# Differential attention scores: three matmuls over 64 rows for each of two maps, in place of two over 128

## The chip, the cores and the metric

The kernel runs on one core of a Trainium2 chip. The metric is the device time of one execution in microseconds (us). A profiled execution of the kernel before is shown beside its times: its span is the time from its first to its last instruction. TensorE is called PE, its weight loads PEld, VectorE DVE, ScalarE ACT, GpSimd POOL and SyncE SP.

## What is computed

The reference is one layer of a decoder trunk with 1024 tokens of width 1024: an RMS norm, one wide input projection, two causal branches of 8 heads each (retention and differential attention), a SiLU gate on each branch, a projection of each branch, a merge by sigmoid gates, and an output projection added to the input. Only the differential attention is touched:

```python
qd = rms_norm(q_d.reshape(B, S, DIFF_HEADS, 2, DIFF_DK), diff_q_norm_g[l])   # DIFF_DK = 64
kd = rms_norm(k_d.reshape(B, S, DIFF_HEADS, 2, DIFF_DK), diff_k_norm_g[l])
...
for i in range(S // Q_BLOCK):                                                # blocks of 128 queries
    ...
    s = jnp.einsum('bqhjd,bkhjd->bhjqk', qb, kb) - slopes[None, :, None, None, None] * dist
    s = jnp.where(dist >= 0, s, -jnp.inf)
    p = jax.nn.softmax(s, axis=-1)
    a = p[:, :, 0] - lam * p[:, :, 1]
    outs.append(jnp.einsum('bhqk,bkhe->bqhe', a, vb))
```

Each head has two score maps, j = 0 and 1. Each is a product of queries and keys over 64 components, and the second softmax is subtracted from the first.

## The kernel before

**Stages.** The input is normalised and transposed, overlapping the first projections; then come the retention branch (to about 293 us), the differential attention (about 293 to 765 us), and the large gate and output products (to the end). All of it runs on one core, and TensorE works on independent pieces of several steps at a time.

**Precision.** A product of two float32 values is made from float32r matmuls. Each operand is split into a high part, rounded to float32r, and a low part, the remainder. The list `PASSES = ((0, 0), (0, 1), (1, 0))` names the three products that are kept: high by high, high by low, low by high.

**The differential stage.** It loops over 8 heads `h` and 8 tiles `t` of 128 queries, 64 steps in all. In a step, `dproj` projects a tile to queries, keys and values: 24 matmuls 384 columns wide into a PSUM bank `z_d` (line 121). The smaller pieces of earlier steps are handed to `after(d, w, fn, key)`: they are issued `d` steps later, between the parts of that step's projection, in the order of `key` (0 to 1 over the step), with `w` as their weight in the spacing. The tile framework then orders the instructions of each engine by a simulated timeline. The pieces of a tile are:

- `mean`, `scale`, `high`, `low` (one step later): the norm of queries and keys and the split. The tile `sp` (named `nsp`) has for each of four 64-wide pieces (query of map 0, query of map 1, key of map 0, key of map 1) the high part in columns 0 to 63 and the low part in columns 64 to 127.
- `d_qkT` (one step later): four transposes of `sp` into one `tr` bank `tq` (line 510). Transposed, rows 0 to 63 hold the high part and rows 64 to 127 the low part of one piece. ACT copies the queries three times into `Q` (lines 514 to 516): as they are, and with the halves exchanged, which needs two copies over 64 rows. DVE copies the keys into the head's `K` (line 517).
- `d_score` (two steps later): for one map `j` and one range of `m` columns of keys (tiles 0 to 3 have one range, tiles 4 to 7 have two), two matmuls over 128 rows into an `s` bank `sps` (line 533). The first adds high by high and low by low, the second, with the halves of the query exchanged, low by high and high by low. DVE adds the distance term and keeps the minimum (line 535), and after the last range ACT takes the exponential (line 539).
- `d_mix` (three steps later), then `d_aT` and `d_pv` (four steps later): the difference of the two maps, its transposes in `tr` banks (`aT`, line 560, copied to `aTs` on ACT or DVE, line 562), and its product with the values (`dops`, line 573). Then `d_norm` and `d_out`, the latter with four more transposes into a `tr` bank (line 610) for each four tiles.

PSUM has eight banks. `NPJ, NS, NTR` share seven of them out to the projections (`pj`), the scores (`s`, also used by retention) and the transposes (`tr`, also used by the first stages); the tag `o` has one.

Of the kernel before, what the change touches and what calls it, by code (L numbers as in the profile page):

```python
# [9 lines left out]
F32 = mybir.dt.float32  # L10
F32R = mybir.dt.float32r
AF = mybir.ActivationFunctionType
ALU = mybir.AluOpType
AX = mybir.AxisListType

P = 128
D = 1024
S = 1024
# [9 lines left out]
FMAX = 3.4028235e38  # L28
NWS = 11
TLS = True  # L30
QSB, KVB = 1, 1
NPJ, NS, NTR = 2, 2, 3
D_F, K_F = (1, 2, 2, 4), (.3, .3, .8, .5)
LAG_S, LAG_PV = 2, 4
K_N = (.1, .25, .4, .55)
D_MIX, K_MIX = 1, .05
K_QK, K_S, L_S, K_PV, L_PV = .9, 0., .8, .1, .8
# [25 lines left out]
def tile_hybrid_block(ctx, tc, x, norm_g, w_in, ret_norm_g, ret_w_o, dq_g, dk_g,  # L63
                      lq1, lk1, lq2, lk2, sub_g, diff_w_o, w_out, consts, out):
    nc = tc.nc
# [11 lines left out]
    def pst(tag, name, bufs=None):  # L77
        bufs = bufs or dict(pj=NPJ, s=NS)[tag]
        return ps.tile([P, 512], F32, tag=tag, name=name, bufs=bufs)
# [7 lines left out]
    def rstd(out_t, ss, pool, name, n, m):  # L87

        ms = pool.tile([P, n], F32, tag="rs_ms", name=f"ms_{name}", bufs=2)
        nc.gpsimd.tensor_scalar(ms, ss, m, EPS, ALU.mult, ALU.add)  # L90
        nc.gpsimd.tensor_tensor(out_t, ms, mh[:, :n], ALU.pow)  # L91
# [5 lines left out]
    def after(d, w, fn, key=1):  # L97

        later.setdefault(clock[0] + d, []).append((w, fn, key))

    PASSES = ((0, 0), (0, 1), (1, 0))
# [140 lines left out]
    def proj(chunk, t, n=512):  # L242
        if t == 3:
            wnext(chunk)
        z = pst("pj", f"z_{chunk}_{t}")
        step(z[:, :n], [hT[k, t // 4] for k in range(NK)], slice((t % 4) * P, (t % 4 + 1) * P),
             W[chunk], slice(0, n))
        return z
# [212 lines left out]
    with tc.tile_pool(name="dp", bufs=2) as dp:  # L461
        ndist = dp.tile([P, S], F32, name="ndist", bufs=1)
# [3 lines left out]
        def dproj(h, t):  # L466
            if t == 0:
                gh = dp.tile([P, 4, 64], F32, tag="gh", name=f"gh{h}")
                nc.gpsimd.tensor_copy(gh[:, 2:4, :], gains[:, 2:4, :])
                nc.gpsimd.tensor_scalar(gh[:, 0:2, :], gains[:, 0:2, :], 2.0 ** (h - 2), None, ALU.mult)  # L470
                heads[h] = dict(V=[], Q={}, sp={}, S={}, st={}, aT={}, o={}, O={}, g=gh)
            hd = heads[h]
            z = proj(f"d{h}", t, 384)
            if t % 4 == 0:
                hd["V"].append(dp.tile([P, 4, P], F32, tag="V", name=f"V{h}{t}", bufs=3))
            zqk = z[:, :256].rearrange("p (a b) -> p a b", b=64)
            sq = dp.tile([P, 4, 64], F32, tag="nsq", name=f"nsq{h}{t}")
            nc.scalar.activation(sq, zqk, AF.Square)
            nc.scalar.activation(hd["V"][t // 4][:, t % 4, :], z[:, 256:384], AF.Copy)  # L479
            ss = dp.tile([P, 8], F32, tag="nss", name=f"nss{h}{t}")  # L480
            sp = hd["sp"][t] = dp.tile([P, 4, P], F32R, tag="nsp", name=f"nsp{h}{t}")

            def mean():
                nc.vector.tensor_reduce(ss[:, :4], sq, AX.X, ALU.add)
                rstd(ss[:, 4:], ss[:, :4], dp, f"n{h}{t}", 4, 1.0 / 64)

            def scale():
                nc.vector.tensor_tensor(sq, zqk, ss[:, 4:].unsqueeze(2).broadcast_to([P, 4, 64]),  # L488
                                        ALU.mult)
                nc.gpsimd.tensor_tensor(sq, sq, hd["g"], ALU.mult)  # L490


            def high():
                nc.scalar.activation(sp[:, :, 0:64], sq, AF.Copy)

            def low():
                nc.vector.tensor_tensor(sp[:, :, 64:128], sq, sp[:, :, 0:64].bitcast(F32),
                                        ALU.subtract)

            for i, fn in enumerate((mean, scale, high, low)):  # L500
                after(1, .01, fn, K_N[i])

        def d_qkT(h, t):
            hd = heads[h]
            sp = hd["sp"].pop(t)
            if t == 0:
                hd["K"] = dp.tile([P, 2, S], F32R, tag="K", name=f"K{h}")
            tp = pst("tr", f"tq{h}{t}", NTR)
            for i in range(4):
                nc.tensor.transpose(tp[:, i * P:(i + 1) * P].bitcast(F32R), sp[:, i, :], identr)  # L510
            tv = tp.rearrange("p (a b) -> p a b", b=P)

            Q = dp.tile([P, 2, 2, P], F32R, tag="Q", name=f"Q{h}{t}", bufs=3)
            nc.scalar.activation(Q[:, :, 0, :], tv[:, 0:2, :], AF.Copy)
            nc.scalar.activation(Q[0:64, :, 1, :], tv[64:P, 0:2, :], AF.Copy)
            nc.scalar.activation(Q[64:P, :, 1, :], tv[0:64, 0:2, :], AF.Copy)  # L516
            nc.vector.tensor_copy(hd["K"][:, :, t * P:(t + 1) * P], tv[:, 2:4, :])
            hd["Q"][t] = Q

        def d_score(h, t, j, f, m):  # L520

            hd = heads[h]
            n = (t + 1) * P
            slope = 2.0 ** -(h + 1)
            if j == 0 and f == 0:
                hd["st"][t] = dp.tile([P, 8], F32, tag="ast", name=f"ast{h}{t}", bufs=5)
            if f == 0:
                hd["S"][t, j] = dp.tile([P, S], F32, tag=f"S{j}", name=f"S{h}{t}{j}", bufs=3 - j)
            st, sb = hd["st"][t], hd["S"][t, j]
            c = slice(m * f, m * f + m)  # L530
            sp = pst("s", f"sps{h}{t}{j}{f}")
            for e in range(2):
                nc.tensor.matmul(sp[:, :m], hd["Q"][t][:, j, e, :], hd["K"][:, j, c],  # L533
                                 start=(e == 0), stop=(e == 1))
            nc.vector.tensor_tensor_reduce(  # L535
                sb[:, c], sp[:, :m], ndist[:, S - n + m * f:S - n + m * f + m], -slope,
                FMAX if f == 0 else st[:, j:j + 1], ALU.add, ALU.min, st[:, j:j + 1])
            if m * f + m == n:
                nc.scalar.activation(sb[:, :n], sb[:, :n], AF.Exp, bias=st[:, j:j + 1], scale=-1.0,  # L539
                                     accum_out=st[:, 2 + j:3 + j])  # L540

        def d_mix(h, t):

            hd = heads[h]
            n = (t + 1) * P
            st, S0, S1 = hd["st"][t], hd["S"][t, 0], hd["S"].pop((t, 1))
            nc.vector.reciprocal(st[:, 4:6], st[:, 2:4])
            nc.vector.scalar_tensor_tensor(st[:, 6:7], st[:, 2:3], st[:, 5:6], nlam,
                                           ALU.mult, ALU.mult)
            nc.vector.scalar_tensor_tensor(S0[:, :n], S1[:, :n], st[:, 6:7], S0[:, :n],  # L550
                                           ALU.mult, ALU.add)
# [54 lines left out]
        def d_out(h, f):  # L606
            O = heads[h]["O"].pop(f)
            tp = pst("tr", f"oT{h}{f}", NTR)
            for b in range(4):
                nc.tensor.transpose(tp[:, b * P:(b + 1) * P], O[:, b, :], ident)  # L610
            oT = dp.tile([P, 512], F32, tag="oT", name=f"doT{h}{f}", bufs=1)
            nc.scalar.activation(oT, tp, AF.Copy, scale=gcol[:, 1, h:h + 1])
            nc.sync.dma_start(ot_d[h][:, f * 512:(f + 1) * 512], oT)

        for h in range(H):
            for t in range(NT):
                dproj(h, t)
                nf = (t + 4) // 4
                after(1, .34, lambda a=(h, t): d_qkT(*a), K_QK)
                for j in range(2):  # L620
                    for f in range(nf):
                        m = (t + 1) * P // nf
                        after(LAG_S, m / 1200, lambda a=(h, t, j, f, m): d_score(*a),
                              K_S + L_S * (j * nf + f) / (2 * nf))
                after(LAG_S + D_MIX, .01, lambda a=(h, t): d_mix(*a), K_MIX)
                nbs = [min(4, t + 1 - 4 * f) for f in range(nf)]
                seq = [(d_aT, f, .116 * nbs[f]) for f in range(nf)]
                seq += [(d_pv, f, .218 * nbs[f]) for f in range(nf)]
                for i, (fn, f, w) in enumerate(seq):
                    after(LAG_PV, w, lambda fn=fn, a=(h, t, f): fn(*a), K_PV + L_PV * i / len(seq))  # L630
                if t % 4 == 3:
                    for i in range(3):
                        after(LAG_PV + D_F[i], .01, lambda a=(h, t // 4, i): d_norm(*a), K_F[i])
                    after(LAG_PV + D_F[3], .46, lambda a=(h, t // 4): d_out(*a), K_F[3])
                tick()
# [345 lines left out]
```

## Time and profile before

| what | value |
|---|---|
| time, median of 3 runs | 1322.15 us (1320.63 to 1325.82) |
| profiled execution, its own time | 1322.55 us |
| its span | 1320.8 us |
| mean granted TensorE clock | 0.985 |
| instructions | 19793 |
| HBM traffic, mean | 128 GB/s |

How to read what follows. In a row of a group, the source line, engine and operation are followed by the output and inputs by their tile names, shapes and count; after the first bar stand the busy time in us and the mean length of one in ns; after the second, the engine's idle time just before them and what ended it. Matmuls are pipelined and their ends are modelled, so a matmul's length is longer than its distance to the next. The chain that ended last is followed back from the last instruction, at each step to what released it or to the instruction before it on its engine.

### The profile page before, as it was taken

What the parts mean: (1) busy time and instruction counts of PE and PEld (TensorE: products, weight loads), DVE (VectorE), ACT (ScalarE), POOL (GpSimd) and SP (SyncE); (2) the same over time, 40 slices, a digit from 0 to 9 for tenths busy, and PEclk for the clock granted to TensorE, in tenths of its full rate; (3) what the DMA queues carried; (4) which work ended last, traced back from release to release, by engine and by line L of the source; (5) the groups of instructions that cost most, each with busy time, mean ns of one, the idle gap of its engine ahead of it and who ended that gap; (6) DMA issues with size and microseconds to landing.
All of it is one profiled execution on the core that took longest, in us unless ns stands there. A gap on an engine that the chain in (4) does not pass through costs nothing.

```text
span 1320.8 us, 19793 instructions
## 1 busy us (share of the span) xinstructions
PE 1264.3 (96%) x6836; PEld 1113.4 (84%) x6836; DVE 950.9 (72%) x2016; ACT 651.4 (49%) x1448; POOL 265.4 (20%) x371
## 2 busy tenths in 40 slices
PE   7999999999999999999999997899989999998698
PEld 5888888889999999999999885687778888876586
DVE  7436435737786877777687838987876699998884
ACT  6235123527575766767676724434454454442420
POOL 3134113323333534243333100000000000012000
PEclk9999999999999999999999998899999999999799
DMA  7202120431010101102020326578876578998963
GB/s 259 66 29 72 57 72 8 125 107 49 9 57 9 57 10 56 55 11 65 9 72 9 120 89 201 189 256 276 298 251 208 160 245 274 301 277 178 253 191 112
DMA packets 157750, 169.95 MB, mean 129 GB/s; under 512 B 9921, under 2 KB 108369, under 8 KB 157649
## 3 DMA queue, kind: packets, MB, share of 16 engines
q1 hardware_dynamic: 154816, 163.68, 38.4%
q0 software_dynamic: 2832, 5.00, 2.6%
q8 instruction: 54, 0.88, 0.3%
q14 instruction: 48, 0.39, 0.1%
HBM read 122.51 MB, written 46.14 MB: 128 GB/s over the span
## 4 chain that ended last, share of the span: by engine, by line
PE 67%; DVE 13%; DMA 11%; issue 4%; ACT 3%; POOL 2%; SPq 1%; DVEq 0%; ACTq 0%; POOLq 0%
PE z_d L121 18%; PE z_rv L121 7%; PE z_rqk L121 6%; PE fb L130 5%; PE sps L533 5%; PE dops L573 5%; PE z_h L130 3%; PE w_h L130 3%; PE aT L560 2%; DMA og<-c_h 2%; PE X_out L130 2%; PE z_out L130 2%; PE w_out L130 2%; PE y_h L130 1%; DMA r_o<-og 1%
## 5 line engine op out<-in xcount | busy, mean ns | idle before, releaser
L121 PE MATMUL z_d<-w_d,hT 128*128 128x384 f32 x1536 | 303.5, 340 | 1.4 <-DVE nsq L488 1.4
L121 PEld LDWEIGHTS z_d<-w_d,hT 128*128 128x128 f32 x1536 | 264.3, 188 | 4.5 <-ACT V L479 1.7
L539 ACT ACTIVATE S<-S,ast 128x256 f32<-128x256 f32 (+7 forms) x128 | 99.0, 774 | 33.4 <-DVE ast L535 32.0
L533 PE MATMUL sps<-K,Q 128*128 128x512 f32 (+5 forms) x384 | 107.5, 363 | 0.5 <-ACT Q L516 0.5
L919 POOL DMA_DIRECT2D md<-c_y x16 | 13.9, 869 | 435.0 <-DVE ls_y L663 372.7
L121 PE MATMUL z_rv<-w_rv,hT 128*128 128x512 f32 x384 | 98.8, 397 | 0.0
L121 PE MATMUL z_rqk<-w_rqk,hT 128*128 128x512 f32 x384 | 94.1, 398 | 0.9 <-ACT hT L283 0.9
L121 PEld LDWEIGHTS z_rqk<-w_rqk,hT 128*128 128x128 f32 x384 | 70.9, 190 | 15.8 <-ACT hT L283 1.6
L573 PE MATMUL dops<-V,aTs 128*128 128x128 f32 x576 | 78.7, 275 | 0.0
L121 PEld LDWEIGHTS z_rv<-w_rv,hT 128*128 128x128 f32 x384 | 68.7, 188 | 11.8
L573 PEld LDWEIGHTS dops<-V,aTs 128*128 128x128 f32 x576 | 76.6, 191 | 2.2 <-ACT aTs L562 0.2
L535 DVE CUSTOM_DVE_ANT_0 S<-sps,ndist 128x512 f32<-128x512 f32 (+5 forms) x128 | 67.9, 533 | 10.4 <-PE sps L533 10.1
L130 PE MATMUL fb<-hT,fw 128*128 128x512 f32 x288 | 71.5, 396 | 0.0
L91 POOL TENSOR_TENSOR nss<-ms_n,mh 128x4 f32<-128x4 f32 x64 | 67.2, 1051 | 4.3
L533 PEld LDWEIGHTS sps<-K,Q 128*128 128x128 f32 x384 | 63.2, 189 | 3.1 <-ACT Q L516 1.5
L130 PEld LDWEIGHTS fb<-hT,fw 128*128 128x128 f32 x288 | 52.7, 188 | 10.2
L490 POOL TENSOR_TENSOR nsq<-nsq,gh 128x256 f32<-128x256 f32 x64 | 47.5, 746 | 63.7 <-DVE nsq L488 62.4
L550 DVE SCALAR_TENSOR_TENSOR S<-S,ast,S 128x128 f32<-128x128 f32 (+3 forms) x64 | 55.5, 868 | 1.2
L130 PE MATMUL z_h<-hT,ls_h 128*128 128x512 f32 x192 | 48.4, 401 | 6.0 <-DVE c_h L810 5.9
L130 PE MATMUL y_h<-t_h,ls_h 128*128 128x512 f32 x192 | 49.0, 398 | 3.3 <-ACT t_h L662 3.3
L662 ACT ACTIVATE ls_h<-s_h 128x512 fp32r<-128x512 f32 x64 | 38.6, 621 | 27.0 <-PE z_h L130 18.6
L130 PE MATMUL w_h<-t_h,l_h 128*128 128x512 f32 x192 | 48.4, 398 | 3.5 <-DVE u_h L822 3.5
(251 smaller groups left out, 2760.3 us busy)
## 6 DMA issues: line engine op xcount, KB each, us to landing
wr_d<-in_w_in_dram SPq DMA_DIRECT2D x96, 128.0 KB, 2.8
ra_h<-in_w_in_dram SPq DMA_DIRECT2D x16, 512.0 KB, 4.2
rb_h<-in_w_in_dram SPq DMA_DIRECT2D x16, 512.0 KB, 5.3
s<-sg SPq DMA_DIRECT2D x32, 256.0 KB, 4.2
fr<-in_w_in_dram SPq DMA_DIRECT2D x12, 512.0 KB, 4.8
first<-ft SPq DMA_DIRECT2D x24, 256.0 KB, 2.0
og<-c_h SPq DMA_DIRECT2D x24, 256.0 KB, 4.4
sg<-c_h SPq DMA_DIRECT2D x24, 256.0 KB, 3.3
```

The costliest lines, as they stand in the source:

```text
L91: nc.gpsimd.tensor_tensor(out_t, ms, mh[:, :n], ALU.pow)
L121: nc.tensor.matmul(o, a[k][:, i0, asl], b[k][:, i1, bsl], start=(k == 0 and j == 0), stop=(k == NK - 1 and j == 2))
L130: nc.tensor.matmul(bank, L[:, i0, j * P:(j + 1) * P], R[:, j, i1, :], start=(start and j == 0 and i == 0), stop=(j == 3 and i == 2), skip_ ...
L490: nc.gpsimd.tensor_tensor(sq, sq, hd["g"], ALU.mult)
L533: nc.tensor.matmul(sp[:, :m], hd["Q"][t][:, j, e, :], hd["K"][:, j, c], start=(e == 0), stop=(e == 1))
L535: nc.vector.tensor_tensor_reduce(sb[:, c], sp[:, :m], ndist[:, S - n + m * f:S - n + m * f + m], -slope, FMAX if f == 0 else st[:, j:j + 1 ...
L539: nc.scalar.activation(sb[:, :n], sb[:, :n], AF.Exp, bias=st[:, j:j + 1], scale=-1.0, accum_out=st[:, 2 + j:3 + j])
L550: nc.vector.scalar_tensor_tensor(S0[:, :n], S1[:, :n], st[:, 6:7], S0[:, :n], ALU.mult, ALU.add)
L560: nc.tensor.transpose(tp[:, b * P:(b + 1) * P], A[:, c:c + P], ident)
L573: nc.tensor.matmul(o[:, :P], aT[:, b, :], hd["V"][f][:, b, :], start=(kb == 0), stop=(kb == t))
L662: nc.scalar.activation(dst_hi, src, AF.Copy)
L919: nc.gpsimd.dma_start(m, t, accum_op=ALU.add)
```

## The change

The halves of the array's rows hold the two maps, where they held the high and the low part of one. `sp` is laid out so that a transposed tile has map 0 in rows 0 to 63 and map 1 in rows 64 to 127: one tile with the high parts and one with the low parts of the queries, and the same for the keys. `Q` is then one copy, half as large. A call of `d_score` covers both maps of a column range: it takes two `s` banks and issues six matmuls over 64 rows, alternating between map 0 in the lower half and map 1 in the upper half, three passes each; low by low is no longer computed. Then follow the reductions and, after the last range, the exponentials of both maps. `NS` goes from 2 to 3 and `NTR` from 3 to 2, and the weights given to `after` follow the new grouping.

```diff
-NPJ, NS, NTR = 2, 2, 3
+NPJ, NS, NTR = 2, 3, 2
...
+            sv = sp.rearrange("p (a h) (b c) -> p a h b c", h=2, b=2)
+            sqv = sq.rearrange("p (a b) c -> p a b c", b=2)
+
             def high():
-                nc.scalar.activation(sp[:, :, 0:64], sq, AF.Copy)
+                nc.scalar.activation(sv[:, :, 0], sqv, AF.Copy)
 
             def low():
-                nc.vector.tensor_tensor(sp[:, :, 64:128], sq, sp[:, :, 0:64].bitcast(F32),
-                                        ALU.subtract)
+                nc.vector.tensor_tensor(sv[:, :, 1], sqv, sv[:, :, 0].bitcast(F32), ALU.subtract)
...
-            Q = dp.tile([P, 2, 2, P], F32R, tag="Q", name=f"Q{h}{t}", bufs=3)
-            nc.scalar.activation(Q[:, :, 0, :], tv[:, 0:2, :], AF.Copy)
-            nc.scalar.activation(Q[0:64, :, 1, :], tv[64:P, 0:2, :], AF.Copy)
-            nc.scalar.activation(Q[64:P, :, 1, :], tv[0:64, 0:2, :], AF.Copy)
+            Q = dp.tile([P, 2, P], F32R, tag="Q", name=f"Q{h}{t}", bufs=3)
+            nc.scalar.activation(Q, tv[:, 0:2, :], AF.Copy)
...
-        def d_score(h, t, j, f, m):
+        def d_score(h, t, f, m):
...
-            sp = pst("s", f"sps{h}{t}{j}{f}")
-            for e in range(2):
-                nc.tensor.matmul(sp[:, :m], hd["Q"][t][:, j, e, :], hd["K"][:, j, c],
-                                 start=(e == 0), stop=(e == 1))
-            nc.vector.tensor_tensor_reduce(
-                sb[:, c], sp[:, :m], ndist[:, S - n + m * f:S - n + m * f + m], -slope,
-                FMAX if f == 0 else st[:, j:j + 1], ALU.add, ALU.min, st[:, j:j + 1])
+            sps = [pst("s", f"sps{h}{t}{j}{f}") for j in range(2)]
+            for i, (i0, i1) in enumerate(PASSES):
+                for j in range(2):
+                    b = slice(64 * j, 64 * j + 64)
+                    nc.tensor.matmul(sps[j][:, :m], hd["Q"][t][b, i0, :], hd["K"][b, i1, c],
+                                     start=(i == 0), stop=(i == 2))
+            for j in range(2):
+                sb = hd["S"][t, j]
+                nc.vector.tensor_tensor_reduce(
+                    sb[:, c], sps[j][:, :m], ndist[:, S - n + m * f:S - n + m * f + m], -slope,
+                    FMAX if f == 0 else st[:, j:j + 1], ALU.add, ALU.min, st[:, j:j + 1])
...
-                for j in range(2):
-                    for f in range(nf):
-                        m = (t + 1) * P // nf
-                        after(LAG_S, m / 1200, lambda a=(h, t, j, f, m): d_score(*a),
-                              K_S + L_S * (j * nf + f) / (2 * nf))
+                for f in range(nf):
+                    m = (t + 1) * P // nf
+                    after(LAG_S, m / 800, lambda a=(h, t, f, m): d_score(*a), K_S + L_S * f / nf)
```

More of the change, by code (lines that the diff above doesn't have):

```diff
@@ L524, in d_score @@
             slope = 2.0 ** -(h + 1)
-            if j == 0 and f == 0:
+            c = slice(m * f, m * f + m)
+            if f == 0:
                 hd["st"][t] = dp.tile([P, 8], F32, tag="ast", name=f"ast{h}{t}", bufs=5)
[L527 to L530, printed above, removed]
-            sp = pst("s", f"sps{h}{t}{j}{f}")
-            for e in range(2):
-                nc.tensor.matmul(sp[:, :m], hd["Q"][t][:, j, e, :], hd["K"][:, j, c],
-                                 start=(e == 0), stop=(e == 1))
-            nc.vector.tensor_tensor_reduce(
-                sb[:, c], sp[:, :m], ndist[:, S - n + m * f:S - n + m * f + m], -slope,
-                FMAX if f == 0 else st[:, j:j + 1], ALU.add, ALU.min, st[:, j:j + 1])
-            if m * f + m == n:
-                nc.scalar.activation(sb[:, :n], sb[:, :n], AF.Exp, bias=st[:, j:j + 1], scale=-1.0,
-                                     accum_out=st[:, 2 + j:3 + j])
+                for j in range(2):
+                    hd["S"][t, j] = dp.tile([P, S], F32, tag=f"S{j}", name=f"S{h}{t}{j}", bufs=3 - j)
+            st = hd["st"][t]
+            sps = [pst("s", f"sps{h}{t}{j}{f}") for j in range(2)]
[4 more added lines that the diff above has]
+                                     start=(i == 0), stop=(i == 2))
+            for j in range(2):
+                sb = hd["S"][t, j]
+                nc.vector.tensor_tensor_reduce(
+                    sb[:, c], sps[j][:, :m], ndist[:, S - n + m * f:S - n + m * f + m], -slope,
+                    FMAX if f == 0 else st[:, j:j + 1], ALU.add, ALU.min, st[:, j:j + 1])
+                if m * f + m == n:
+                    nc.scalar.activation(sb[:, :n], sb[:, :n], AF.Exp, bias=st[:, j:j + 1],
+                                         scale=-1.0, accum_out=st[:, 2 + j:3 + j])
         def d_mix(h, t):
```

## The prediction

> **What bounds the kernel now.** I read the page first: the engine totals, the chain that ended last, and the groups of the score lines.
>
> ```profile
> span 1320.8 us, 19793 instructions
> PE 1264.3 (96%) x6836; PEld 1113.4 (84%) x6836; DVE 950.9 (72%) x2016; ACT 651.4 (49%) x1448; POOL 265.4 (20%) x371
> PE 67%; DVE 13%; DMA 11%; issue 4%; ACT 3%; POOL 2%; SPq 1%; DVEq 0%; ACTq 0%; POOLq 0%
> L533 PE MATMUL sps<-K,Q 128*128 128x512 f32 (+5 forms) x384 | 107.5, 363 | 0.5 <-ACT Q L516 0.5
> L535 DVE CUSTOM_DVE_ANT_0 S<-sps,ndist 128x512 f32<-128x512 f32 (+5 forms) x128 | 67.9, 533 | 10.4 <-PE sps L533 10.1
> ```
>
> TensorE is busy nearly always and carries two thirds of the chain. The change touches the stage of the differential attention, from about 293 to 765 us, so the view by windows comes second, once for everything and once for the score tile `sps` alone.
>
> ```profile
> 293.00:765.00 472.00, 470.83 (x3090) 455.20 (x3089) 356.01 (x1031) 325.85 (x861) 166.14 (x243) 1.00 0.14 42
> 293.00:765.00 472.00, 107.48 (x384) 63.24 (x384) 108.99 (x192) 1.00 0.14 42
> ```
>
> The columns are length, PE, weight loads, DVE, ACT and POOL in the first row, and length, PE, weight loads and DVE in the second; then the granted clock (1.00), DMA share and GB/s. PE is busy 470.83 of 472 us, DVE 356, ACT 326. In this stage a microsecond of TensorE issue added or removed is a microsecond of the span, and work of DVE or ACT costs something only where a matmul waits for it.
>
> A matmul's busy time overlaps the next one's, so the price of one is the distance between them. I take that from the chain in order of time (start, length, what) and from the timeline of PE and of its weight loads (PEld), whose length of a merged row runs from the first start to the last end.
>
> ```profile
> 266.37 5.46 PE fb L130 x24
> 503.56 2.09 PE z_d L121 x12
> 508.32 0.35 PE sps L533 x2
> 494.53 0.30 PE sps L533 x2
> 527.92 0.24 PE sps L533 x2
> 505.65 0.89 PE dops L573 x8
> 531.11 0.30 PEld L533 LDWEIGHTS sps<-K,Q 128*128 128x128 f32 x2
> 503.23 2.10 PEld L121 LDWEIGHTS z_d<-w_d,hT 128*128 128x128 f32 x12
> 501.99 0.19 PEld L533 LDWEIGHTS sps<-K,Q 128*128 128x128 f32 x1 [0.36 <-ACT Q L516]
> ```
>
> 512 columns cost 5.46/24 = 0.227 us, 384 columns 2.09/12 = 0.174 us. The line through them gives 0.147 for 320, 0.20 for 448 and 0.12 for 256; the score pairs agree (384 wide 0.35/2, 320 wide 0.30/2). By the line 128 columns would cost 0.07, but they cost 0.12 in scores and 0.89/8 = 0.11 in `dops`. The weight load sets that: one load alone takes 0.19, two in a row span 0.30, so a second load follows 0.11 after the first. Where the stream is longer, loads keep its distance, (2.10 - 0.19)/11 = 0.174, and are hidden. So the price of a matmul today is the larger of its stream and 0.11 us.
>
> **The change part by part.** The counts come from the groups by shape, in the window of the stage.
>
> ```profile
> L533 PE MATMUL sps<-K,Q 128*128 128x512 f32 x96 | 32.7, 422 | 0.0
> L533 PE MATMUL sps<-K,Q 128*128 128x384 f32 x96 | 26.2, 361 | 0.5 <-ACT Q L516 0.5
> L533 PE MATMUL sps<-K,Q 128*128 128x448 f32 x64 | 19.2, 382 | 0.0
> L533 PE MATMUL sps<-K,Q 128*128 128x320 f32 x64 | 15.7, 322 | 0.0
> L533 PE MATMUL sps<-K,Q 128*128 128x256 f32 x32 | 7.5, 314 | 0.0
> L533 PE MATMUL sps<-K,Q 128*128 128x128 f32 x32 | 6.3, 284 | 0.0
> ```
>
> *1, matmuls and loads.* Before: 96 x 0.227 + 96 x 0.174 + 64 x 0.20 + 64 x 0.147 + 32 x 0.12 + 32 x 0.11 = 68.1 us. After, 384 matmuls of 128 rows become 576 of 64 rows: 288 couples, one matmul in rows 0 to 63 for map 0 and one in rows 64 to 127 for map 1, and there are 576 loads. Per width there are 3/4 as many couples as there were matmuls. All 6836 matmuls traced use 128 rows, so no row shows whether two of 64 rows run side by side. Bounds: wholly side by side, loads too, 3/4 of 68.1 = 51.1 us, a gain of 17.0; one after another, 6/4 of it = 102.1 us, a loss of 34.0. I take matmuls side by side (different rows, different PSUM banks) but loads in turn, by the nearest row: loads on one path 0.11 apart. Then a couple cannot cost less than two loads, 0.22 us, and only the 512 wide ones are bound by their stream: 72 x 0.227 + 216 x 0.22 = 63.9 us. Term: -4.2 us.
>
> *2, going into and out of 64 rows.* There are 96 groups of scores (8 heads, 4 tiles with one column range and 4 with two), each an island among 128-row matmuls: 192 changes, if the scheduler leaves the groups whole (each break adds two). Today a load is pulled under the running matmul. Whether a load for 64 rows is pulled under a matmul over all rows, and the reverse, no row shows. What one uncovered load costs does stand in the trace: the load at 501.99, late by 0.36 us, and the matmul it feeds, beside a matmul of the same 384 columns in the stream:
>
> ```profile
> 501.99 0.44 PE L533 MATMUL sps<-K,Q 128*128 128x384 f32 x1
> 501.44 0.34 PE L121 MATMUL z_d<-w_d,hT 128*128 128x384 f32 x1
> ```
>
> 0.44 - 0.34 = 0.10 us. Bounds per change: 0, if the load is pulled ahead as now; or 0.10 and the rest of the matmul in flight, 0.34 - 0.174 = 0.166, if the array must run empty first, 0.27 together. I take 0.10, the measured row. Term: 192 x 0.10 = +19.2 us, between 0 and +51.
>
> A rule of the Trainium skill speaks against this change. TensorEngine Tiling (Array Packing), Key Properties, says that changing the tiling mode, unlike changing the tile within a mode, drains TensorE. No row of before can show it; by it the term would be the upper end, +51.
>
> *3, the query copy.* Three ACT copies become one.
>
> ```profile
> L514 ACT ACTIVATE Q<-tq 128x256 fp32r<-128x256 f32 x64 | 24.8, 387 | 7.0 <-PE tq L510 6.8
> L515 ACT ACTIVATE Q<-tq 64x256 fp32r<-64x256 f32 x64 | 24.4, 382 | 0.9
> L516 ACT ACTIVATE Q<-tq 64x256 fp32r<-64x256 f32 x64 | 24.1, 377 | 0.8
> PEld sps L533 <- ACT Q L516: 1.5, 3, 0.6
> PE sps L533 <- ACT Q L516: 0.5, 2, 0.2
> PEld sps L533 <- ACT Q L514: 0.4, 1, 0.4
> ```
>
> ACT loses 24.4 + 24.1 = 48.5 us of work, all beside TensorE; Q is ready 0.76 us earlier. What matmuls wait for it is at most 1.5 + 0.5 + 0.4 = 2.4 us. Term: -2.4, at worst 0. The copies of the split (`high`, `low`) keep their counts and sizes: 0, hidden under PE.
>
> *4, PSUM banks.* `tr` falls from 3 to 2, so a transpose waits for the copy two before it. The trace has such waits with three banks: first the waits in total, then two pieces of the chain.
>
> ```profile
> PEld tq L510 <- ACT aTs L562: 1.7, 4, 0.4
> PE tq L510 <- ACT aTs L562: 0.7, 4, 0.2
> 501.97 0.59 ACT aTs L562
> 502.61 0.54 PE tq L510 x4
> ```
>
> Together 2.4 us. The bank of `tq` comes free 0.76 us sooner (part 3), and ready projection matmuls can fill a wait. I take a doubling, +2.4. Bounds: 0, and one wait of 0.59 in each of the 32 steps with two column ranges, +19. `s` rises from 2 to 3, but each call takes two at once: its second bank is one that the call before used, and the two reductions that free them now come together. PE has no visible wait for `s` today; a reduction takes 0.53 us (the L535 row) against the 2.9 us between two calls of a tile (0.4 of 472/64). The cover is that distance; gone, it would cost one reduction at most, in part of the 96 groups. I take 0. The DMAs, their sizes and the queues of SP and POOL are unchanged: 0.
>
> **Sum.** -4.2 + 19.2 - 2.4 + 2.4 = +15.0 us. The profiled execution took 1322.55 us (span 1320.8), 0.4 above the median 1322.15; so 1337.6 in its terms, **1337 us** for the median, 1.1% slower.
>
> **The rivals.**
>
> *Faster.* The loads of the two halves also go side by side and the changes cost next to nothing: -17.0 - 2.4 + 2.4, about 1305, or 1314 with 0.05 a change. For it: loads hide under matmuls everywhere today. Against: two loads are 0.11 apart. It decides at 17.0/192 = 0.089 us a change: below that the kernel gains, above it loses. The Trainium skill, TensorE: Matmul & The Clock Gate, Part 3, speaks for it: matmuls in different row groups start within about 4 ns, and loads overlap matmuls of another row group. No 64-row matmul runs here, so that is unseen.
>
> *No change.* One side of part 1 with the other of part 2: loads side by side but 0.10 a change, -17.0 + 19.2, 1324; or loads in turn and free changes, -4.2, 1318.
>
> *The array empties at every change.* 0.27 x 192 = 51, so 1369 with loads in turn and 1356 with loads side by side. For it: a matmul ends 0.166 after the next could start, so there is something to wait for. Against: nothing shown. The Trainium skill's sentence on draining, named in part 2 (TensorEngine Tiling (Array Packing), Key Properties), is the rule for this one.
>
> *No running side by side.* The change then does not do what it says: +34.0 by part 1, 1356, before any cost of changes. Against: the couples share neither rows nor banks. For: nothing in before has ever run so.
>
> **How the numbers follow.** Forecast with neighbours (1329 to 1350): 0.32. Faster: 0.31. No change: 0.15. Emptying array: 0.13. No running side by side: 0.09. Half a percent (6.6 us) is about what can be told from no change: faster 0.31, same 0.15, slower 0.32 + 0.13 + 0.09 = 0.54. The range must reach from the faster rival to the dearest ones: 1305 to 1370 leaves out under 0.2. The forecast's own range is 1329 to 1350.
>
> **What would show it.** Two score matmuls of a couple that start within hundredths of a microsecond show matmuls side by side; starts a stream apart show the last rival. Two score loads 0.11 apart on PEld confirm part 1's floor, and 384 wide couples then cost 0.22 of the chain, not 0.174. For part 2, the first 64-row matmul after a 128-row one, and the first 128-row one after, should last 0.10 longer than in the stream, or start that much late; nothing there means the faster rival, 0.27 the emptying one. For part 4, look at waits of transposes on `aTs` and `K`. The forecast is wrong above all if changes are free, or if loads of different rows do not queue.

## The result: 3.5% slower, and the profile after

The changed kernel takes 1367.91 us (median of 4 runs, 1365.46 to 1371.48) against 1321.39 for the kernel before on the same chip: ratio 1.0348, 95% interval 1.0314 to 1.0382, or 46.5 us lost. The forecast was 1337; the time lies inside the range, but the loss is three times the one forecast.

The page of the changed kernel, in the lines that answer to those of before (line 533 is now 535, 573 is 577, 560 is 564, 510 is 512), and behind them one row of the page of before:

```profile
span 1363.7 us, 19981 instructions
PE 1313.7 (96%) x7028; PEld 1110.7 (81%) x7028; DVE 947.7 (69%) x2016; ACT 601.1 (44%) x1320; POOL 266.4 (20%) x371
PE 73%; DVE 10%; DMA 10%; issue 3%; ACT 1%; POOL 1%; SPq 0%; DVEq 0%; POOLq 0%; ACTq 0%
L535 PE MATMUL sps<-K,Q 64*128 64x512 f32 (+5 forms) x576 | 107.9, 371 | 0.0
L535 PEld LDWEIGHTS sps<-K,Q 64*128 64x128 f32 x576 | 62.3, 184 | 29.0 <-issue 12.2
```
```profile
L533 PEld LDWEIGHTS sps<-K,Q 128*128 128x128 f32 x384 | 63.2, 189 | 3.1 <-ACT Q L516 1.5
```

ACT lost its 50 us of work, as the prediction said, and no gain of it shows. The busy time of the score matmuls is nearly unchanged (107.5 before, 107.9 now), although there are 576 instead of 384: a part of them overlap one another. New is the idle time of the load path before the score loads: 29.0 us, where it was 3.1 before. The largest part, 12.2 us, is put down to "issue", that is, to nothing the profile shows. Pieces of the chain, in order of time, show what it is.

```profile
523.38 0.17 PE z_d L121
523.56 0.64 PE sps L535 x3
525.79 0.72 PE sps L535 x5
527.80 0.44 PE dops L577 x4
528.25 0.72 PE sps L535 x3
528.97 0.64 PE dops L577 x4
```

The score pieces at 525.79 and 528.25 are both 384 columns wide. The first is a whole group of both maps (the chain counts five of its six matmuls), the second three matmuls of one map; both take 0.72 us. Three streams of 384 columns are 3 x 0.174 = 0.52, so each piece pays 0.20 on top. Whatever follows pays again: four `dops` matmuls take 0.64 behind the scores and 0.44 behind a projection. The timeline of PE and of its loads around the piece at 525.79:

```profile
525.28 0.19 PEld L121 LDWEIGHTS z_d<-w_d,hT 128*128 128x128 f32 x1
525.72 0.47 PEld L535 LDWEIGHTS sps<-K,Q 64*128 64x128 f32 x6 [0.25 <-issue]
526.43 0.42 PEld L614 LDWEIGHTS oT<-ident,O 128*128 128x128 f32 x4 [0.25 <-issue]
525.72 0.79 PE L535 MATMUL sps<-K,Q 64*128 64x384 f32 x6
```

Six matmuls over 64 rows go through in three streams, and six weight loads of 0.18 us lie within 0.47: the halves load and stream side by side. But the first load for 64 rows, and the first for 128 rows behind them, each come after 0.25 us in which the load path stood still. Before, loads were pulled under the running matmul.

I divided the distances between the ends of successive matmuls of the stage, all of them, from the first `z_d` to the last `fb`, into the stream (width price of the prediction, 0.11 us for 128 columns, the traced 0.072 for `tq`), what a matmul costs beyond it where the row count changes, and the other excess ("waits"). In us:

| kernel | other streams | score streams | changes: number, cost | waits | stage |
|---|---|---|---|---|---|
| before | 431.7 | 68.2 | 0 | 12.7 | 512.6 |
| after | 431.7 | 74.3 | 266, 49.0 | 7.2 | 562.2 |

The stage grew by 49.6: +49.0 for changes, +6.1 for score streams, -5.5 for waits. The span of the profiled execution grew by only 42.9, because after spent 520.6 us behind the stage where before spent 528.4. The experiments below spent between 523.6 and 531.0 there, apart from the three with one transpose bank (543 to 546); what moves this part, no run separates.

Two things beside the price went against the change. The scheduler did not keep the groups whole: in the program, 76 of the 133 runs of score matmuls hold three matmuls of one map alone, with projections, transposes or `dops` between the two maps. That makes 266 changes instead of 192, and only 163 of 288 couples side by side (ends within 0.024 us of each other).

### The profile page after: what moved, and what is told of

It is laid out like the page before. It is cut to its first block, busy times and chain, and to the rows that moved or that the text cites. A ratio compares the mean times of both kernels' runs of the same rounds, so it can differ in the third digit from the quotient of the medians.

```text
span 1363.7 us, 19981 instructions
## 1 busy us (share of the span) xinstructions
PE 1313.7 (96%) x7028; PEld 1110.7 (81%) x7028; DVE 947.7 (69%) x2016; ACT 601.1 (44%) x1320; POOL 266.4 (20%) x371
## 4 chain that ended last, share of the span: by engine, by line
PE 73%; DVE 10%; DMA 10%; issue 3%; ACT 1%; POOL 1%; SPq 0%; DVEq 0%; POOLq 0%; ACTq 0%
PE z_d L121 20%; PE sps L535 7%; PE z_rv L121 6%; PE z_rqk L121 6%; PE dops L577 5%; PE fb L130 5%; PE z_h L130 3%; PE w_h L130 3%; PE aT L564 3%; PE X_out L130 2%; PE z_out L130 2%; PE w_out L130 2%; DMA og<-c_h 2%; PE tq L512 2%; PE y_h L130 1%
## 5 line engine op out<-in xcount | busy, mean ns | idle before, releaser
L121 PE MATMUL z_d<-w_d,hT 128*128 128x384 f32 x1536 | 306.6, 345 | 0.7 <-DVE nsq L488 0.7
L121 PEld LDWEIGHTS z_d<-w_d,hT 128*128 128x128 f32 x1536 | 261.3, 188 | 13.1 <-issue 9.0
L535 PE MATMUL sps<-K,Q 64*128 64x512 f32 (+5 forms) x576 | 107.9, 371 | 0.0
L535 PEld LDWEIGHTS sps<-K,Q 64*128 64x128 f32 x576 | 62.3, 184 | 29.0 <-issue 12.2
L577 PE MATMUL dops<-V,aTs 128*128 128x128 f32 x576 | 84.3, 280 | 1.5 <-ACT aTs L566 1.5
L90 POOL TENSOR_SCALAR ms_n<-nss 128x4 f32<-128x4 f32 x64 | 17.6, 275 | 200.7 <-DVE nss L484 199.2
L554 DVE SCALAR_TENSOR_TENSOR S<-S,ast,S 128x128 f32<-128x128 f32 (+3 forms) x64 | 53.5, 837 | 1.0
L539 DVE CUSTOM_DVE_ANT_0 S<-sps,ndist,ast 128x320 f32<-128x320 f32 (+3 forms) x64 | 41.1, 646 | 17.7 <-PE sps L535 17.3
L665 DVE TENSOR_TENSOR ls_h<-s_h,ls_h 128x512 fp32r<-128x512 f32 x64 | 43.3, 685 | 12.8 <-ACT ls_h L664 12.8
```

What stands on the lines that cost most here:

```text
L121: nc.tensor.matmul(o, a[k][:, i0, asl], b[k][:, i1, bsl], start=(k == 0 and j == 0), stop=(k == NK - 1 and j == 2))
L535: nc.tensor.matmul(sps[j][:, :m], hd["Q"][t][b, i0, :], hd["K"][b, i1, c], start=(i == 0), stop=(i == 2))
L539: nc.vector.tensor_tensor_reduce(sb[:, c], sps[j][:, :m], ndist[:, S - n + m * f:S - n + m * f + m], -slope, FMAX if f == 0 else st[:, j:j ...
L577: nc.tensor.matmul(o[:, :P], aT[:, b, :], hd["V"][f][:, b, :], start=(kb == 0), stop=(kb == t))
L665: nc.vector.tensor_tensor(dst_lo, src, dst_hi.bitcast(F32), ALU.subtract)
```

## The experiments

Theory 1: each change between 64 and 128 rows costs about 0.18 us, whatever is computed. Theory 2: the new bank counts and the order cost the time. Theory 3: the loss is matmuls over 64 rows without a partner.

**The price of a change, in the kernel before.** The second of two score matmuls uses rows 0 to 63 alone; nothing else moves.

```diff
             for e in range(2):
-                nc.tensor.matmul(sp[:, :m], hd["Q"][t][:, j, e, :], hd["K"][:, j, c],
+                b = slice(0, 64) if e else slice(0, P)
+                nc.tensor.matmul(sp[:, :m], hd["Q"][t][b, j, e, :], hd["K"][b, j, c],
                                  start=(e == 0), stop=(e == 1))
```

> The kernel before with the second of each two score matmuls over rows 0 to 63 alone (the low part of the keys times the high part of the queries is left out). Same matmuls, widths, loads and banks; each pair now holds one excursion into 64 rows, 192 excursions and 384 changes. Theory 1 at 0.18 us a change: +69 us, about 1390. At 0.10 a change (the prediction's value): +38, 1360. At 0.27 (the upper bound): +104, 1425. If a change costs nothing: 1321.

Measured: 1391.09 us against 1322.64, ratio 1.0505 (1.0475 to 1.0535), +68.5 us. Then both matmuls over rows 0 to 63 (`hd["Q"][t][0:64, j, e, :]`, `hd["K"][0:64, j, c]`):

> The kernel before with both score matmuls over rows 0 to 63 (the products of the other half are left out): twice the 64-row matmuls of the run above, in about 182 runs, so about as many changes, 364. Theory 1 (the price is of the change): +66 us, about 1387, no more than the run above. Rival (the price sits on each 64-row matmul): twice the loss of the run above, +139, about 1460.

Measured: 1384.88, ratio 1.0466 (1.0441 to 1.0491), +62.2 us. Twice as many 64-row matmuls cost a little less, in 182 runs instead of 192 excursions. So the price sits on the change and not on the matmul. The chain at the same place of the program, in the kernel before, with the second matmul changed, and with both changed:

```profile
389.88 0.36 PE sps L533 x2
390.23 0.44 PE aT L560 x4
390.67 0.36 PE sps L533 x2
391.03 0.29 PE tq L510 x4
```
```profile
403.91 0.55 PE sps L534 x2
404.46 0.59 PE aT L561 x4
405.05 0.55 PE sps L534 x2
405.60 0.47 PE tq L510 x4
```
```profile
403.12 0.55 PE sps L533 x2
403.66 0.59 PE aT L560 x4
404.25 0.54 PE sps L533 x2
404.79 0.47 PE tq L510 x4
```

Each score pair pays 0.19, on going in, and whatever follows pays 0.15 to 0.18 on going out; in the last two kernels the rows are the same, though the change lies inside the pair in one and before it in the other. By the division above, 384 changes cost 71.9 us and 364 cost 68.3: 0.187 each.

**No change of rows.** The changed kernel with its six score matmuls over all 128 rows, which sums both maps in each score (`hd["Q"][t][:, i0, :]`, `hd["K"][:, i1, c]`):

> The changed kernel with the same six score matmuls over all 128 rows (both maps are summed, so the scores differ): no change of mode and nothing side by side. Theory 1: +34 us of stream against before and nothing for changes, less some 3 us for the single query copy, about 1352. Theory 2 (banks and order): above 1368, since banks and order stay and the stream grows by 28 us against the changed kernel, 1396. Theory 3 (the loss is lack of running side by side): 1368 + 28 = 1396 as well.

Measured: 1351.12 against 1323.4, ratio 1.02 (1.0183 to 1.0217). It issues six full streams where the changed kernel has some couples, and is still 17 us faster than that. Theory 1 had said 1352, theories 2 and 3 1396. Its trace has the same 133 runs of score matmuls as the changed kernel, so the broken order does not cost the time by itself. Then three matmuls in place of six (two into the first bank, one into the second):

```diff
             for i, (i0, i1) in enumerate(PASSES):
-                for j in range(2):
-                    b = slice(64 * j, 64 * j + 64)
-                    nc.tensor.matmul(sps[j][:, :m], hd["Q"][t][b, i0, :], hd["K"][b, i1, c],
-                                     start=(i == 0), stop=(i == 2))
+                j = i // 2
+                nc.tensor.matmul(sps[j][:, :m], hd["Q"][t][:, i0, :], hd["K"][:, i1, c],
+                                 start=(i != 1), stop=(i != 0))
```

> The changed kernel with three score matmuls over all 128 rows in place of six (two into the first bank, one into the second; half of the products is left out): the stream of couples that run wholly side by side, without a change of mode. Theory 1: 17 us below before and some 3 us for the query copy, about 1302. Theory 2: 1368 less 23 us of stream, about 1345.

Measured: 1307.81, ratio 0.9879 (0.9865 to 0.9894), -15.6 us. That is what couples would bring if changes were free; the prediction's bound was 17.0.

**The banks.** The kernel before with `NPJ, NS, NTR = 2, 3, 2`:

> The kernel before with the changed kernel's PSUM banks alone (three for scores, two for transposes). Theory 1 (changes of mode): 1321, within 5 us. Theory 2 (banks): 1345 or more. The prediction had put this term at +2.4 us with an upper bound of 19.

Measured: 1330.67, ratio 1.0057 (1.0036 to 1.0078): +8 us, more than theory 1 allowed and far less than theory 2 needs. PE waits for copies of `aT`, as this answer on waits shows; before has no such wait of `dops`:

```profile
PE dops L573 <- ACT aTs L562: 8.4, 6, 1.4
```

In the changed kernel the same wait is 1.5 us. That slower matmuls give the copies time would explain it, but no run shows it apart.

**Whole groups by a fourth score bank: misses.** With `NPJ, NS, NTR = 2, 4, 1` the scheduler keeps 96 whole groups.

> The changed kernel with four score banks and one bank for transposes, so that both maps of a call find a free bank and the six matmuls of a call stay together: 96 runs of score matmuls in place of 133. Theory 1 (each entry into and exit from 64-row matmuls costs about 0.18 us, as the trace of the changed kernel shows): 192 changes x 0.18 = 35 us, all 288 couples side by side, 17 us less stream than before, so about 1336, plus what one transpose bank costs. Theory 2 (the banks cause the loss: transposes wait): slower than the changed kernel, over 1370. Theory 3 (the only loss is couples that are not formed): 73.8 - 51.1 = 22.7 us below the changed kernel, 1345, and couples in the trace all start together.

> The kernel before with the same four score banks and one transpose bank: the control of the run above. Theory 1: the banks cost little, 1320 to 1330. Theory 2: 1345 or more, since with one bank each transpose waits for the copy before it.

> The changed kernel with four score banks, one transpose bank, and both column ranges of a tile in one group of twelve matmuls: 64 groups, 128 changes, all couples side by side. Theory 1: 128 x 0.18 = 23 us for changes, 17 us less stream, about 12 us below the run with 96 groups on the same banks. Theory 3 (couples alone count): the same as that run.

The last one issues both column ranges of a tile as one group of twelve (`for f in reversed(range(nf))` around the passes, four banks taken ahead of it) with the same bank counts. Measured: 1424.5, 1434.58 and 1448.25 us, ratios 1.0757 (1.0735 to 1.0778), 1.0823 (1.0791 to 1.0855) and 1.0941 (1.0912 to 1.0969). The last is 24 us above the first, where theory 1 had it 12 below and theory 3 the same. These bank counts cost 111 us in the kernel before: TensorE now waits in the stage, and the clock granted there (from 293 to 765 us) is 0.98 in that run, 0.96 and 0.93 in the other two, where it was 1.00 before. So these three say nothing on the price of changes. Here theory 2 was right, for a count that the change does not use. The longest waits of PE in the kernel before with these counts:

```profile
PE sps L533 <- DVE K L517: 18.8, 16, 1.7
PE z_d L121 <- DVE nsq L488: 11.4, 19, 1.5
PE aT L560 <- ACT aTs L562: 10.6, 16, 1.5
```

**Whole groups on the bank counts of before.** The two score banks of a call become one tile of two banks, so that a call starts when both are free; retention keeps its two `s` banks in a pool that closes ahead of the stage, and `tr` has its three again.

```diff
-            sps = [pst("s", f"sps{h}{t}{j}{f}") for j in range(2)]
+            two = psd.tile([P, 2, 512], F32, tag="sd", name=f"sps{h}{t}{f}", bufs=1)
+            sps = [two[:, j, :] for j in range(2)]
```

> The changed kernel with the bank counts of before (two for scores, three for transposes), where the two score banks of a call are one tile of two banks, so that a call starts only when both are free: 96 whole groups of six, 192 changes in place of 266, all 288 couples side by side. Theory 1 (a change costs 0.186 us, the mean of the entries and exits in the run with both score matmuls over half of the rows): 192 x 0.186 = 35.7, less 17.0 of stream, about 1340 (1334 to 1345). Theory 3 (the scheduler's broken groups do not matter, or the price is not of the change): 1365 as the changed kernel. If the single pair of banks makes matmuls wait for the reductions: above 1345, with waits of score matmuls on the reductions in the trace.

Measured: 1333.07 against 1323.56, ratio 1.0076 (1.0052 to 1.0101). The program has 96 groups of six, and 279 of 288 couples are side by side in the trace (ends within 0.024 us; the starts of all 288 lie within 0.03). Against its own runs of before, 9.5 of the 46.5 us lost are left: whole groups, with the transposes' third bank back, recover 37 us. The kernel is still slower than before. The time is below the 1334 to 1345 expected. Its control, with three matmuls over 128 rows as above:

> The kernel of the run above with three score matmuls over all 128 rows in place of the three couples (half of the products is left out): the same banks, the same stream of 51.1 us, no change of mode. Theory 1: about 1305, and the run above is slower than this one by 192 x 0.186 = 35.7 us (33 to 38). If couples do not run wholly side by side, the difference is larger; if part of the loss is banks or order, this run stays above 1315.

Measured: 1309.15, ratio 0.9891 (0.9868 to 0.9915). The difference is 23.9 us, not 35.7. The division of both traces shows why:

| kernel | other streams | score streams | changes: number, cost | waits | stage |
|---|---|---|---|---|---|
| couples | 431.2 | 53.5 | 192, 37.1 | 5.8 | 527.6 |
| three full | 431.2 | 51.1 | 0 | 21.6 | 504.0 |

The changes do cost 37.1 us (0.193 each), but without them score matmuls wait, in this answer for a result that DVE still owes:

```profile
PE sps L541 <- DVE ast L558: 9.0, 6, 1.5
```

The waits are 15.8 us longer than with couples, so part of the price is paid in time that would otherwise be waited.

**The order within a group.** The same kernel, with the matmuls of a group kept in the order map 0 three times, then map 1 three times.

> The kernel with the pair of banks with the six matmuls of a group kept in the order map 0, 0, 0, map 1, 1, 1: the same 192 changes, but only the last of map 0 and the first of map 1 are neighbours in different halves. Theory 1: if those two run side by side, the stream is 5/6 of 102.3 = 85.2 us, 34 us above the kernel with couples, about 1374; if they do not, 51 above, about 1391. If the order within a group does not matter (matmuls of the other half are pulled ahead): as the kernel with couples, about 1340.

Measured: 1334.53, ratio 1.008 (1.0057 to 1.0104): the same as with couples, the third outcome. The program has all 96 groups in this order, yet the trace shows 274 couples side by side by the same measure, and the starts of all 288 lie within 0.04 us. The timeline of PE for one group 448 wide, first alternating, then map by map:

```profile
466.74 0.88 PE L542 MATMUL sps<-K,Q 64*128 64x448 f32 x6
```
```profile
466.83 0.88 PE L542 MATMUL sps<-K,Q 64*128 64x448 f32 x6
```

Both take as long as three streams, 3 x 0.20, the 0.10 of a late load and the last matmul's tail. In the second the first matmul of map 1 starts 0.01 us after the first of map 0, ahead of two that stand before it in the program. What keeps halves apart in the changed kernel is thus not the order of the six but the 128-row matmuls that the scheduler put between the two maps.

## Why the prediction was wrong

*Part 2 is the step that failed.* It took 0.10 us a change and 192 changes, +19.2. The traces show 0.184 (49.0/266) and 266 changes, +49.0. The row that I took, a load that came late, is one half of the price: a matmul behind an uncovered load ends 0.10 later. The other half is that the load starts only after the stream of the matmul in flight has ended. For the piece at 525.79, the timeline of PE has that matmul as the second of this row:

```profile
525.27 0.51 PE L121 MATMUL z_d<-w_d,hT 128*128 128x384 f32 x2
```

The second starts one stream after the first, at 525.27 + 0.174 = 525.45. The first 64-row load starts at 525.72, 0.27 us after it, where the next matmul of a stream starts 0.174 after: 0.09 to 0.10 late. The delay behind the stream does not grow with the width in flight: in the trace of after its median is 0.095 behind `dops` (128 columns), 0.094 behind `z_d` (384) and 0.091 behind `fb` (512). My upper bound had put the whole modelled tail, 0.166, there; that was too much. So the rival "the array empties at every change", which had 0.13, comes nearest, at two thirds of its price. What happens inside the array in the 0.09 us, no trace shows. The Trainium skill's sentence that a change of tiling mode drains TensorE (TensorEngine Tiling (Array Packing), Key Properties) fits the trace: 0.14 to 0.20 us for a change of mode in these kernels, and none between halves.

*The number of changes.* "If the scheduler leaves the groups whole" was written as a condition and then costed at nothing. With three score banks for calls that take two, the second map often has no free bank, and its matmuls are issued later: 74 more changes and 125 couples not formed. By the two tables that is 49.0 - 37.1 = 11.9 us of changes and 74.3 - 53.5 = 20.8 us of stream, together 32.7 of the 37 us that whole groups brought back; the waits, with the third transpose bank, differ by only 1.4.

*Part 1.* "Loads in turn" was wrong: loads of different halves run side by side, and whole couples cost 53.5 us, near the 51.1 of the lower bound (3/4 of the stream). The row of 0.11 between loads is of loads to the same rows. The term came to +6.1 for another reason, the couples not formed.

*Parts 3 and 4.* The query copy and the banks were put at -2.4 and +2.4. Waits fell by 5.5 in all, which fits a longer PE path that hides them, though no run separates the two parts; the banks alone cost the kernel before 8 us, inside the bounds of 0 and 19.

*The rivals.* "No running side by side" is refuted by the 0.72 us of the whole group. For the faster rival, the price of a change at which the gain is gone was 0.089; it was measured at twice that. A group of one column range saves one stream, at most 0.227 us, and pays two changes, 0.37 to 0.39 on average: no such group of this kernel can gain by itself. It would have to hold two of the widest ranges, which takes four score banks, and the only version tried with four left one bank to the transposes.

## What to carry to other kernels

Count the islands before counting the streams saved: in this kernel a stretch of 64-row matmuls among 128-row ones costs about 0.38 us, whatever is in it, so it must save more than that by itself. Where a bound of a rival decides the sign, the number of times it is paid deserves a look at what the scheduler can do with the waits that the change adds: here one bank too few added 40% to the number. And a price taken from a nearby row covers what that row contains; a late load shows the load, not the emptying ahead of it.

## What the runs showed of the hardware

Halves of the array run as if each had a queue of its own: in 96 groups issued as three matmuls of one half and then three of the other, 274 of 288 couples still ran together, at the same time as alternating ones (1334.53 and 1333.07 us). Weight loads of the two halves overlap as well, six of 0.18 us in 0.47. By the division, a change of the row count costs the same going in (0.19) whether one, two or six matmuls follow (the kernel before with the second matmul changed, with both changed, and whole groups); going out it costs 0.20 ahead of a projection or `dops`, and less ahead of transposes, 0.15 (`aT`) and 0.14 (`tq`, whose whole piece of four is 0.18 longer).
